# The out-projection as seven products per block pair, with weight sums prepared early in DRAM

## Chip, cores and metric

One core of a Trainium2 chip runs the whole kernel. The metric is the device time of one execution in microseconds (us); less is better. The engines are TensorE (PE, with its weight loads shown apart as PEld), VectorE (DVE), ScalarE (ACT), GpSimd (POOL) and SyncE (SP), from whose queue all DMAs are issued here.

## What is computed

One layer of a hybrid decoder: 2048 tokens of width 1024, an input projection shared by two head groups (8 heads of latent attention, and a gated linear recurrence, HGRN2), gates, one output projection, residual and a final RMSNorm.

```python
h = rms_norm(x, ln_g[l])
proj = h @ w_in[l]
q_lat, kv_lat, k_rope, g_mla, hq, hf, hi, g_hg = jnp.split(proj, split_pts, axis=-1)
y_mla = mla_group(...) * jax.nn.silu(g_mla)        # causal attention, (2048, 512)
y_hg = hgrn2_group(...) * jax.nn.silu(g_hg)        # chunkwise recurrence, (2048, 512)
y = jnp.concatenate([y_mla, y_hg], axis=-1) @ w_out[l]     # (2048, 1024) @ (1024, 1024)
x = x + y
return rms_norm(x, final_norm_g)
```

All is float32. A large matmul is made of three: each operand is split into a high part (a cast to the fp32r type) and a low part (the rest), and high x high, high x low and low x high are accumulated in PSUM (`mm3`, lines 67 to 70).

## The kernel before

Three stages follow one another. **Stage 1** (to about 700 us) projects and runs HGRN2: token chunks of 512, feature groups of 256 columns; each `hg_unit` (line 440) has a first level, five more levels, `inter`, `outputs` and `norm`. A level subtracts on POOL (L447, L468), takes exponentials on ACT (L470, L471), multiplies on DVE (L480, L481) and ends in small matmuls (L486). The latent projections `lat_q` (L249) and `lat_kv` (L314) are merged with the second half of the units: `merge` (L140) spreads the items of its lists evenly over one another, and `merge(U[7:], lat_q(0, hA))` (L658), `merge(U[16:], lat_kv(0, hA))` (L666) and `merge(U[16:], lat_q(1, hB))` (L673) are the places that the change adds to.

**Stage 2** is attention: 8 heads of 8 steps of 256 queries. The loop at L1026 merges, in step n, the scores of step n + 1 (`stage_a`, L859: three matmuls per chunk, row minimum on DVE, exponential on ACT), the transposes and value products of step n (`stage_b`, L905: four transposes into a PSUM bank, cast on ACT L932, subtraction on DVE L933, products L947 and L948), and the preparation of the next head (`prep`, L778, by a plan by hand at L989 to L1002). Each step stores its 64 rows of `y` to DRAM (L962). In the step of number 4 of the last head (`WOUT`, L38) `load_wout` (L974) closes the pool `lat` of the latents and splits `w_out` into the room: 4 loads of 1 MB, per 128 rows a cast on ACT (L984) and a subtraction on POOL or DVE (L985).

**Stage 3** is the out-projection (L1042 to L1079): 16 blocks of 128 tokens. A block loads 512 KB of `y` (L1047), splits it (L1048, L1049), loads `x` (L1051), and for each half of 512 columns runs 8 x 3 matmuls into a PSUM bank; DVE adds the residual (L1062), ACT squares with a sum (L1063), POOL takes the power (L1072), ACT scales one half (L1073), DVE the other (L1074), and SP stores 512 KB (L1079). The last block's second half is cut in two.

The program is written in this order, but a scheduler that goes by the order of writing as priority and by its own time estimates sets the order on each engine, so that work of a later place can stand among the work of an earlier one: out-projection matmuls do so from 1224 us on. PSUM has 8 banks: 3 `mm`, 3 `tp`, 1 `a`, 1 `b`.

Of the kernel before, what the change touches and what calls it, by code (L numbers as in the profile page):

```python
# [57 lines left out]
def hybrid_kernel(ctx: ExitStack, tc: tile.TileContext, x, x_t, positions, ln_g, w_in, q_a_norm_g, w_q_b,  # L58
# [719 lines left out]
    def prep(h):  # L778
# [52 lines left out]
        def query(c):  # L831
# [5 lines left out]
            qf = wk.tile([128, 512], F32, tag="qf", bufs=1, name="qf")  # L837
# [1 line left out]
            qh = wk.tile([128, 512], F32R, tag="qh", bufs=2, name="qh")
            ql = wk.tile([128, 512], F32R, tag="ql", bufs=2, name="ql")  # L840
# [133 lines left out]
    def load_wout():  # L974
        p2r.close()
        wo = p2r.enter_context(tc.tile_pool(name="wo", bufs=1, side="right"))
        for k2 in range(KT // 2):
            wr = wk.tile([128, 2, D], F32, tag="vp", name="vp")
            DMA.dma_start(wr, w_out[k2 * 256:(k2 + 1) * 256, :].rearrange("(k p) n -> p k n", p=128))
            for j in range(2):  # L980
                k = 2 * k2 + j
                a = wo.tile([128, D], F32R, name=f"wo_hi{k}")
                b = wo.tile([128, D], F32R, name=f"wo_lo{k}")
                A.copy(a, wr[:, j])  # L984
                (V if k == 0 else G).tensor_tensor(b, wr[:, j], f32(a), ALU.subtract)  # L985
                w_hi.append(a)
                w_lo.append(b)
# [123 lines left out]
```

## Time and profile before

| | us |
|---|---|
| median of 3 runs (lowest, highest) | 1419.92 (1417.84, 1420.91) |
| the profiled execution, its own time | 1418.87 |
| its span, first to last instruction | 1417.1 |
| PE busy in it | 1387.7 |
| DVE, ACT, POOL busy | 958.6, 881.2, 464.8 |
| mean granted TensorE clock | 0.990 |

The page gives busy time, not useful work: a matmul's listed duration is a latency, and matmuls overlap, so a rate is read from how many start in a stretch, or from the distance of two equal events. What bounds a stretch is read from which engine is full there and which one waits.

### The profile page before, as it was taken

What the parts mean: (1) busy time and instruction counts of PE and PEld (TensorE: products, weight loads), DVE (VectorE), ACT (ScalarE), POOL (GpSimd) and SP (SyncE); (2) the same over time, 40 slices, a digit from 0 to 9 for tenths busy, and PEclk for the clock granted to TensorE, in tenths of its full rate; (3) what the DMA queues carried; (4) which work ended last, traced back from release to release, by engine and by line L of the source; (5) the groups of instructions that cost most, each with busy time, mean ns of one, the idle gap of its engine ahead of it and who ended that gap; (6) DMA issues with size and microseconds to landing.
All of it is one profiled execution on the core that took longest, in us unless ns stands there. A gap on an engine that the chain in (4) does not pass through costs nothing.

```text
span 1417.1 us, 25792 instructions
## 1 busy us (share of the span) xinstructions
PE 1387.7 (98%) x9258; PEld 1263.5 (89%) x9258; DVE 958.6 (68%) x2425; ACT 881.2 (62%) x1796; POOL 464.8 (33%) x635
## 2 busy tenths in 40 slices
PE   8999999999999999999899999999999999999998
PEld 7899879989899988998889898999999998888887
DVE  6547855595845845658388889898889889743333
ACT  6565575456862647355388778778777878732232
POOL 3123613083121622237252425233342525411010
PEclk9999999999999999999989999999999999999999
DMA  7211211215411112111630000100010103244442
GB/s 230 75 48 46 75 53 31 67 42 172 138 46 34 54 52 82 38 42 44 194 73 18 19 22 13 24 13 22 13 26 11 25 22 107 74 144 143 134 148 104
DMA packets 100576, 96.30 MB, mean 68 GB/s; under 512 B 31200, under 2 KB 88800, under 8 KB 100320
## 3 DMA queue, kind: packets, MB, share of 16 engines
q1 hardware_dynamic: 100448, 94.65, 22.7%
q8 instruction: 73, 1.20, 0.4%
q14 instruction: 55, 0.45, 0.1%
HBM read 68.41 MB, written 25.17 MB: 66 GB/s over the span
## 4 chain that ended last, share of the span: by engine, by line
PE 85%; DVE 5%; POOL 3%; ACT 2%; issue 2%; DMA 2%; SPq 0%; POOLq 0%; DVEq 0%; ACTq 0%
PE ps_mm L68 14%; PE ps_mm L69 14%; PE ps_mm L70 14%; PE ps_tp L929 8%; PE ps_a L948 5%; PE ps_a L947 4%; PE ps_mm L881 4%; PE ps_mm L883 4%; PE ps_mm L882 4%; PE ps_b L70 2%; PE ps_b L68 2%; PE ps_b L69 2%; PE ps_a L486 2%; PE ps_b L486 1%; POOL dd L468 1%
## 5 line engine op out<-in xcount | busy, mean ns | idle before, releaser
L68 PE MATMUL ps_mm<-w,hh 128*128 128x256 f32 (+3 forms) x896 | 268.3, 299 | 0.0
L69 PE MATMUL ps_mm<-w,hh 128*128 128x256 f32 (+3 forms) x896 | 263.9, 295 | 0.0
L70 PE MATMUL ps_mm<-w,hl 128*128 128x256 f32 (+3 forms) x896 | 263.0, 294 | 0.0
L933 DVE TENSOR_TENSOR pl<-ps_tp,ph 128x512 fp32r<-128x512 f32 (+1 forms) x288 | 184.6, 655 | 33.3 <-ACT ph L932 32.6
L932 ACT CAST ph<-ps_tp 128x512 fp32r<-128x512 f32 (+1 forms) x288 | 154.4, 565 | 60.2 <-PE ps_tp L929 46.7
L68 PEld LDWEIGHTS ps_mm<-w,hh 128*128 128x128 f32 x896 | 170.1, 190 | 0.7
L69 PEld LDWEIGHTS ps_mm<-w,hh 128*128 128x128 f32 x896 | 169.8, 189 | 0.4
L70 PEld LDWEIGHTS ps_mm<-w,hl 128*128 128x128 f32 x896 | 169.3, 189 | 0.1
L929 PE MATMUL ps_tp<-ident,sn 128*128 128x128 f32 x1088 | 167.9, 274 | 0.8 <-ACT sn L895 0.8
L895 ACT ACTIVATE sn<-sn,mx 128x128 f32<-128x128 f32 (+15 forms) x128 | 154.6, 1208 | 21.2 <-DVE mx L890 20.8
L947 PE MATMUL ps_a<-ph,vp 128*128 128x256 f32 x576 | 155.5, 290 | 0.0
L948 PE MATMUL ps_a<-pl,vp 128*128 128x256 f32 x576 | 147.1, 288 | 0.2 <-DVE pl L933 0.2
L468 POOL TENSOR_TENSOR dd<-G 128x512 f32<-128x512 f32 x80 | 92.8, 1164 | 142.9 <-DVE qd L481 106.9
L929 PEld LDWEIGHTS ps_tp<-ident,sn 128*128 128x128 f32 x1088 | 126.8, 140 | 8.8 <-ACT sn L895 1.3
L881 PE MATMUL ps_mm<-k_hi,qh 128*128 128x512 f32 (+3 forms) x320 | 130.8, 409 | 0.5 <-DVE mx L890 0.2
L886 DVE TENSOR_SCALAR_CACHE_REDUCE sn<-ps_mm,mx 128x512 f32<-128x512 f32 (+3 forms) x192 | 111.5, 581 | 10.9 <-PE ps_mm L883 8.8
L883 PE MATMUL ps_mm<-k_hi,ql 128*128 128x512 f32 (+3 forms) x320 | 116.5, 364 | 1.4 <-DVE ql L842 1.4
L882 PE MATMUL ps_mm<-k_lo,qh 128*128 128x512 f32 (+3 forms) x320 | 116.1, 363 | 0.0
L914 POOL TENSOR_SCALAR gp<-gate,ri 128x64 f32<-128x64 f32 x128 | 56.7, 445 | 180.9 <-DVE ri L897 159.7
L230 DVE SCALAR_TENSOR_TENSOR w<-wr,lng,w 128x256 fp32r<-128x256 f32 (+3 forms) x168 | 89.3, 574 | 39.4 <-ACT w L229 39.4
L948 PEld LDWEIGHTS ps_a<-pl,vp 128*128 128x128 f32 x576 | 109.0, 189 | 6.0 <-DVE pl L933 1.2
L947 PEld LDWEIGHTS ps_a<-ph,vp 128*128 128x128 f32 x576 | 108.9, 189 | 5.8 <-ACT ph L932 0.6
(275 smaller groups left out, 3348.5 us busy)
## 6 DMA issues: line engine op xcount, KB each, us to landing
wr<-in_w_in SPq DMA_DIRECT2D x68, 256.0 KB
yl<-y_d SPq DMA_DIRECT2D x16, 512.0 KB
vp<-in_x SPq DMA_DIRECT2D x16, 512.0 KB
out<-sn SPq DMA_DIRECT2D x15, 512.0 KB
xt<-in_x SPq DMA_DIRECT2D x8, 512.0 KB
xs<-in_x_t SPq DMA_DIRECT2D x8, 512.0 KB
y_d<-yt SPq DMA_DIRECT2D x16, 256.0 KB
gate<-gate_d SPq DMA_DIRECT2D x8, 512.0 KB
```

What stands on the lines that cost most here:

```text
L68: PE.matmul(ps, l_hi, r_hi, start=start, stop=False)
L69: PE.matmul(ps, l_hi, r_lo, start=False, stop=False)
L70: PE.matmul(ps, l_lo, r_hi, start=False, stop=stop)
L881: PE.matmul(p[:, :w], qh[:, qs], kh[:, ks], start=True, stop=False)
L882: PE.matmul(p[:, :w], qh[:, qs], kl[:, ks], start=False, stop=False)
L883: PE.matmul(p[:, :w], ql[:, qs], kh[:, ks], start=False, stop=True)
L895: A.activation(sn[:, :nk], sn[:, :nk], AF.Exp, bias=mx[:, kc:kc + 1], scale=-1.0, accum_out=rs)
L929: PE.transpose(tp[:, o:o + 128], prow[i][:, (kb + u) * 128:(kb + u + 1) * 128], ident)
L932: A.copy(ph[:, :w], tp[:, :w])
L933: V.tensor_tensor(pl[:, :w], tp[:, :w], f32(ph[:, :w]), ALU.subtract)
L947: PE.matmul(dst, vv, ph[:, rng], start=st_, stop=False)
L948: PE.matmul(dst, vv, pl[:, rng], start=False, stop=en)
```

## The change

The 2048 x 1024 by 1024 x 1024 product is taken in pairs of token blocks. For a pair, y is seen as a 2 x 2 matrix of [128 tokens, 512 features] quarters a11, a12 (first block), a21, a22 (second), and w_out as four 512 x 512 quarters b11 to b22. Strassen's scheme in Winograd's form takes seven products in place of eight, with four sums of the left quarters (s1 to s4) and four of the right (t1 to t4).

- `wout_sums` computes and splits the seven right operands in eight pieces in stage 1 (lines 658, 666 and 673 get a third list) and stores them to seven DRAM tensors of 2 MB. It uses the buffers `xs` (3) and `xt` (2) of that stage.
- `load_wout` is gone. From step 3 of the last head on (`WOUT = 3`) the sets are loaded into the room of `lat`: one in each of steps 3, 4 and 6, two in step 5; the last two go, in the last step, into the room of the pool `big`, which now also holds the key, query and value buffers of attention and is closed there.
- Stage 3 has 8 pairs. `pair_operands` loads 1 MB of y and 1 MB of x per pair and makes the seven left operands; `pair_products` runs seven products of 4 x 3 matmuls, accumulating in four PSUM banks (three `mm`, one `tp`) that stay open; two are seeded by an ACT copy from another bank, and one matmul each opens banks b and c once.
- The output is formed in place in the x tile.

```diff
-WOUT = 4
+WOUT = 3
...
+    SETS = ("b11", "t1", "t2", "b21", "t3", "b22", "t4")
+    w_d = {name: dram.tile([128, 2, 4, 512], F32R, name="wd_" + name) for name in SETS}
...
+    def wout_sums(kk, ch):
+        ns = slice(ch * 256, ch * 256 + 256)
+        wr = st.tile([128, 2, 2, 256], F32, tag="xs", bufs=3, name="ws")
+        for g in range(2):
+            r0 = g * 512 + kk * 128
+            DMA.dma_start(wr[:, g], w_out[r0:r0 + 128, :].rearrange("p (c n) -> p c n", c=2)[:, :, ns])
+
+        def split(src, names):
+            hl = st.tile([128, 2, 2, 256], F32R, tag="xs", bufs=3, name="whl")
+            n = len(names)
+            A.copy(hl[:, 0, :n], src)
+            V.tensor_tensor(hl[:, 1, :n], src, f32(hl[:, 0, :n]), ALU.subtract)
+            for i, name in enumerate(names):
+                DMA.dma_start(f32(w_d[name][:, :, kk, ns]), f32(hl[:, :, i]))
+
+        t = st.tile([128, 4, 256], F32, tag="xt", name="xt")
+        G.tensor_tensor(t[:, 0], wr[:, 0, 1], wr[:, 0, 0], ALU.subtract)
+        G.tensor_tensor(t[:, 1], wr[:, 1, 1], t[:, 0], ALU.subtract)
+        G.tensor_tensor(wr[:, 0, 1], wr[:, 1, 1], wr[:, 0, 1], ALU.subtract)
+        G.tensor_tensor(t[:, 2], wr[:, 1, 0], t[:, 1], ALU.subtract)
+        split(wr[:, :, 0], ("b11", "b21"))
+        split(wr[:, :, 1], ("t3", "b22"))
+        split(t[:, 0:2], ("t1", "t2"))
+        split(t[:, 2:3], ("t4",))
+
+    sums = [lambda kk=kk, ch=ch: wout_sums(kk, ch) for kk in range(4) for ch in range(2)]
...
-    merge(U[7:], lat_q(0, hA))
+    merge(U[7:], lat_q(0, hA), sums[0:3])
...
-    merge(U[16:], lat_kv(0, hA))
+    merge(U[16:], lat_kv(0, hA), sums[3:6])
...
-    merge(U[16:], lat_q(1, hB))
+    merge(U[16:], lat_q(1, hB), sums[6:8])
...
+    ORDER = (("a11", "b11", "a"), ("s1", "t1", "e"), ("s2", "t2", "b"), ("a12", "b21", "a"),
+             ("s3", "t3", "b"), ("s4", "b22", "c"), ("a22", "t4", "b"))
+    def wload(pool, name):
+        wset[name] = pool.tile([128, 2, 4, 512], F32R, name=name + "s")
+        DMA.dma_start(f32(wset[name]), f32(w_d[name]))
...
+        def split(name, src):
+            hi, lo = o[name] = operand(name)
+            A.copy(hi, src)
+            V.tensor_tensor(lo, src, f32(hi), ALU.subtract)
...
+        def total(name, x0, x1, op):
+            t = o["f" + name] = fin.tile([128, 4, 128], F32, tag="ss", bufs=3, name="ss")
+            V.tensor_tensor(t, x0, x1, op)
+            split(name, t)
...
-        if n == (HEADS - 1) * STEPS + WOUT:
+        first = n - ((HEADS - 1) * STEPS + WOUT)
+        if first == 0:
             run(side)
-            side = []
-            load_wout()
+            side = [open_wout, early("b11")]
+        elif first > 0 and n < len(seq) - 1:
+            side = side + [early(name) for name in {1: ("t1",), 2: ("t2", "b21"), 3: ("t3",)}[first]]
+        elif n == len(seq) - 1:
+            side = [open_late] + pair_operands(0)[:4] + [late("b22"), late("t4")]
...
+    acc = {"a": mmb(), "e": mmb(), "b": mmb(), "c": tpb()}
+    for key_ in "bc":
+        PE.matmul(acc[key_], wset["b11"][:, 0, 0, 0:128], wset["b11"][:, 0, 0], start=True, stop=True)
...
+        def product(i, ns=slice(0, 512)):
+            a, w, bk = ORDER[i]
+            (ah, al), wt, p = o[a], wset[w], acc[bk][:, ns]
+            for k in range(4):
+                first = i < 2 and k == 0
+                PE.matmul(p, ah[:, k], wt[:, 0, k, ns], start=first, stop=False, skip_group_check=True)
+                PE.matmul(p, ah[:, k], wt[:, 1, k, ns], start=False, stop=False, skip_group_check=True)
+                PE.matmul(p, al[:, k], wt[:, 0, k, ns], start=False, stop=k == 3, skip_group_check=True)
...
+        def after(i):
             if i == 0:
+                A.copy(acc["b"], acc["a"])
+            elif i == 1:
+                add(0, H1, acc["e"])
+                add(1, H1, acc["e"])
+            elif i == 2:
+                A.copy(acc["c"], acc["b"])
+            elif i == 3:
+                add(0, H0, acc["a"])
+                done(0, H0, True)
+            elif i == 4:
+                add(1, H1, acc["b"])
+                done(1, H1, True)
+            elif i == 5:
+                add(0, H1, acc["c"])
+                done(0, H1, False)
+                finish(0, H0, H1)
+            elif not last:
+                add(1, H0, acc["b"])
+                done(1, H0, False)
+                finish(1, H1, H0)
```

Here `add` is the DVE addition of a bank to the x tile, `done` the square with its sum and, for one half, the multiplication by the final gain, `finish` power, scaling and store.

## Rows read from the trace of the kernel before

**Rows 1.** The page, part 1: busy time, share, instructions.
```profile
PE 1387.7 (98%) x9258; PEld 1263.5 (89%) x9258; DVE 958.6 (68%) x2425; ACT 881.2 (62%) x1796; POOL 464.8 (33%) x635
```
**Rows 2.** The page, part 4: the last chain's shares by engine.
```profile
PE 85%; DVE 5%; POOL 3%; ACT 2%; issue 2%; DMA 2%; SPq 0%; POOLq 0%; DVEq 0%; ACTq 0%
```
**Rows 3.** Out-projection: busy time by stretch (columns above it); SP's store issues.
```profile
core 0: us, PE busy (x) PEld busy (x) DVE busy (x) ACT busy (x) POOL busy (x), PEclk, DMA share, GB/s
1300.00:1350.00 50.00, 50.00 (x222) 41.38 (x222) 18.08 (x27) 14.72 (x28) 5.22 (x9) 1.00 0.44 142
...
1305.05 0.34 SPq L1079 DMA_DIRECT2D out<-sn  x1
...
1315.93 0.34 SPq L1079 DMA_DIRECT2D out<-sn  x1
```
**Rows 4.** Busy time by stretch, HGRN2 beside latent projections; columns as in rows 3.
```profile
140.00:160.00 20.00, 18.22 (x138) 17.84 (x137) 19.20 (x40) 12.64 (x38) 16.24 (x20) 0.91 0.08 27
160.00:180.00 20.00, 20.00 (x137) 16.93 (x136) 11.09 (x28) 9.71 (x25) 7.96 (x13) 1.00 0.36 106
...
300.00:320.00 20.00, 17.39 (x140) 15.73 (x138) 18.41 (x36) 10.17 (x31) 16.63 (x23) 1.00 0.14 48
...
475.00:495.00 20.00, 18.67 (x153) 18.16 (x153) 17.62 (x42) 10.98 (x33) 16.42 (x19) 1.00 0.12 41
```
**Rows 5.** One of three matmul lines, both banks: ns min/median/max, first and last start.
```profile
L68 PE MATMUL ps_mm<-wo_hi,yh x176: 278/389/481, 1224.1 to 1407.5; 128*128 128x512 f32 x168, 128*128 128x256 f32 x8
...
L68 PE MATMUL ps_b<-wo_hi,yh x88: 283/389/397, 1249.1 to 1410.4; 128*128 128x512 f32 x80, 128*128 128x256 f32 x8
```
**Rows 6.** Groups by line over the span: busy us, mean ns, idle before.
```profile
L814 POOL TENSOR_TENSOR vp<-vs,vp 128x256 fp32r<-128x256 f32 x24 | 17.4, 737 | 21.8 <-ACT vp L813 21.8
...
L841 ACT CAST qh<-qf 128x512 fp32r<-128x512 f32 x32 | 19.9, 622 | 0.7 <-DVE qf L838 0.6
...
L1062 DVE TENSOR_TENSOR vp<-ps_mm,vp 128x512 f32<-128x512 f32 (+1 forms) x22 | 14.9, 676 | 25.1 <-PE ps_mm L70 23.8 <-DMA vp<-in_x 1.2
...
L1074 DVE SCALAR_TENSOR_TENSOR sn<-vp,rxp,ks 128x512 f32<-128x512 f32 x16 | 12.0, 751 | 10.8 <-POOL rxp L1072 10.8
L1067 DVE TENSOR_TENSOR vp<-vp,ks 128x512 f32<-128x512 f32 x16 | 11.1, 692 | 15.4 <-ACT sn L1063 15.4
```
**Rows 7.** One tile's instructions, w_out's halves: ns min/median/max, first and last start.
```profile
L984 ACT CAST wo_hi<-vp x8: 1044/1051/1057, 1185.4 to 1220.2; 128x1024 fp32r<-128x1024 f32 x8
L985 POOL TENSOR_TENSOR wo_lo<-vp,wo_hi x7: 2393/2405/2474, 1187.5 to 1222.7; 128x1024 fp32r<-128x1024 f32 x7
L985 DVE TENSOR_TENSOR wo_lo<-vp,wo_hi x1: 1225/1225/1225, 1186.5 to 1186.5; 128x1024 fp32r<-128x1024 f32 x1
```
**Rows 8.** Busy time by stretch, attention; last, of instructions on tile yh alone (no POOL).
```profile
1100.00:1150.00 50.00, 50.00 (x344) 45.87 (x343) 42.90 (x140) 41.83 (x91) 22.84 (x32) 1.00 0.12 30
...
1187.00:1197.00 10.00, 9.13 (x52) 6.78 (x50) 9.85 (x29) 9.63 (x18) 7.53 (x7) 1.00 0.63 192
...
1224.00:1262.00 38.00, 38.00 (x221) 33.12 (x219) 17.77 (x35) 16.62 (x35) 5.96 (x9) 1.00 0.24 76
...
1224.00:1262.00 38.00, 24.65 (x76) 13.75 (x77) 1.23 (x1) 1.69 (x2) 1.00 0.24 76
```
**Rows 9.** POOL's and DVE's timelines, 144 to 149 us; one line's ns min/median/max.
```profile
144.15 3.66 POOL L468 TENSOR_TENSOR dd<-G 128x512 f32<-128x512 f32 x3
...
144.16 0.41 DVE L481 TENSOR_TENSOR qd<-rq,dd 128x256 f32<-128x256 f32 x1
...
146.79 1.30 DVE L481 TENSOR_TENSOR qd<-rq,dd 128x256 f32<-128x256 f32 x1
...
L481 DVE TENSOR_TENSOR qd<-rq,dd x80: 407/417/1311, 81.5 to 651.9; 128x256 f32<-128x256 f32 x80
```
**Rows 10.** Busy time by stretch while w_out is loaded; columns as in rows 3.
```profile
1178.00:1181.00 3.00, 3.00 (x21) 2.67 (x20) 2.34 (x11) 2.85 (x8) 2.05 (x5) 1.00 0.92 289
```
**Rows 11.** Timeline at the end: the last matmul and the last store's issue.
```profile
1410.63 0.28 PE L70 MATMUL ps_b<-wo_hi,yl 128*128 128x256 f32 x1
...
1413.95 0.38 SPq L1076 DMA_DIRECT2D out<-sn  x1
```

More of the change, by code (lines that the diff above doesn't have):

```diff
@@ L767, in hybrid_kernel @@
     wk = p2.enter_context(tc.tile_pool(name="wk", bufs=2, side="left"))
-    big = p2.enter_context(tc.tile_pool(name="big", bufs=1, side="left"))
     wk2 = p2.enter_context(tc.tile_pool(name="wk2", bufs=2, side="left"))
+    fin = p2.enter_context(tc.tile_pool(name="fin", bufs=1, side="left"))
+    p2k = ExitStack()
+    big = p2k.enter_context(tc.tile_pool(name="big", bufs=1, side="left"))
     k_hi1 = big.tile([128, S], F32R, name="k_hi1")
@@ L836, in query @@
                 mm3(p, wqh[:, k], wql[:, k], q_hi[:, k, sl], q_lo[:, k, sl], k == 0, k == 1)
[L837 removed]
+            qf = big.tile([128, 512], F32, tag="qf", bufs=1, name="qf")
             V.tensor_tensor(qf, p, csT[:, sl], ALU.mult)
[L839 to L840 removed]
+            qh = big.tile([128, 512], F32R, tag="qh", bufs=2, name="qh")
+            ql = big.tile([128, 512], F32R, tag="ql", bufs=2, name="ql")
             A.copy(qh, qf)
@@ L972, in hybrid_kernel @@
     w_hi, w_lo = [], []
-    def load_wout():
-        p2r.close()
[L976 to L987, printed above, removed]
+    ORDER = (("a11", "b11", "a"), ("s1", "t1", "e"), ("s2", "t2", "b"), ("a12", "b21", "a"),
+             ("s3", "t3", "b"), ("s4", "b22", "c"), ("a22", "t4", "b"))
@@ new lines, in hybrid_kernel, with open_wout @@
+    wset = {}
+    ys = [{} for _ in range(NBLK // 2)]
+    o_pools = {}
+    def wload(pool, name):
+        wset[name] = pool.tile([128, 2, 4, 512], F32R, name=name + "s")
+        DMA.dma_start(f32(wset[name]), f32(w_d[name]))
+    def open_wout():
+        p2r.close()
+        o_pools["wo"] = p2r.enter_context(tc.tile_pool(name="wo", bufs=1, side="right"))
+        o_pools["fng"] = fng = fin.tile([128, D], F32, name="fng")
+        DMA.dma_start(fng, bass.AP(tensor=final_norm_g.tensor, offset=final_norm_g.offset, ap=[[0, 128], [1, D]]))
@@ new lines, in early, with open_late, late, operand @@
+    def early(name):
+        return lambda: wload(o_pools["wo"], name)
+    def open_late():
+        p2k.close()
+        o_pools["ln"] = ln.enter_context(tc.tile_pool(name="ln", bufs=1, side="right", reuse_waits="tile"))
+    def late(name):
+        return lambda: wload(o_pools["ln"], name)
+    ln = ExitStack()
+    def operand(name):
+        if name in ("a11", "s1", "s2", "a12"):
+            t = o_pools["ln"].tile([128, 2, 4, 128], F32R, tag=name, name=name)
+            return t[:, 0], t[:, 1]
+        if name in ("s3", "s4"):
+            t = wk2.tile([128, 2, 4, 128], F32R, tag="gate", name="gate")
+            return t[:, 0], t[:, 1]
+        return (wk2.tile([128, 4, 128], F32R, tag="ph", bufs=3, name="ph"),
+                wk2.tile([128, 4, 128], F32R, tag="pl", bufs=3, name="pl"))
@@ L1081, in hybrid_kernel @@
+    run(pair_operands(0)[4:])
+    for b in range(NBLK // 2):
+        merge(pair_products(b), pair_operands(b + 1) if b + 1 < NBLK // 2 else [])
+    ln.close()
+    p2.close()
     p2r.close()
-    p2.close()
 def kernel(x, positions, ln_g, w_in, q_a_norm_g, w_q_b, kv_a_norm_g, w_kv_b, hg_lower_bounds, hg_norm_g,
```

104 lines of the change are left out of this document (63 added, 41 removed).

## Prediction

> **What bounds the kernel now.** I read the busy table of the whole span first, then the shares of the chain that ended last, then busy time by stretch, and last the single rows that price an edit. TensorE is busy 98% of the span and carries 85% of the chain, DVE and POOL 8% together [rows 1, 2]. So the time is TensorE's work plus the few places where it is kept waiting, and an edit is worth what it takes from TensorE's queue or adds to those places. The out-projection is the purest case: in a 50 us stretch TensorE never stops at full clock, while DVE is busy 18 us, ACT 15 us, and DMA a share of 0.44 [rows 3]. There two stores of finished blocks are issued 10.88 us apart [rows 3], and a block is 2 halves x 8 tiles x 3 matmuls = 48 of 512 columns: 0.2267 us each. (The listed 389 ns is a pipelined latency, not a price.)
>
> The places where TensorE is kept waiting matter for what the change adds. In the HGRN2 stage there are stretches, about 140 to 160, 300 to 320 and 475 to 495 us, where it is busy only 17.4 to 18.7 of 20 us while DVE is busy 17.6 to 19.2 and POOL 16.2 to 16.6; 20 us later it is full again and DVE has fallen to 11 [rows 4].
>
> **The change, part by part.**
>
> *Out-projection.* Before, 248 matmuls of 512 columns and 16 of 256 start from each of three lines [rows 5]: 744 and 48, worth 768 of the long ones (16 blocks x 48). After, 8 block pairs x 7 products x 4 tiles x 3 = 672, plus 2 that only open two banks. That takes 94 away: 94 x 0.2267 = **-21.3 us**, all on the path, since nothing else bounds this stage. What must still fit in a pair's 84 x 0.2267 = 19.0 us: DVE does 7 subtractions and 4 operand sums of two SBUF tiles (11 x 0.69), 6 additions out of PSUM (6 x 0.68), 2 multiplications (2 x 0.69), 2 final scalings (2 x 0.75) and two tiny steps: 14.9 us. ACT does 7 casts, 2 bank copies, 4 squares and 2 scalings, 15 x 0.62 = 9.3 us [rows 6]. DMA moves 3 MB per pair as before. DVE goes from 37% to 78%, and TensorE stays the bound.
>
> *Bank copies.* Two copies PSUM to PSUM per pair are new (a to b after product 1, b to c after product 3), and TensorE waits for each. No row shows such a copy; the nearest is a cast at 0.62 us [rows 6]. One whole product, 12 x 0.2267 = 2.7 us, lies between each copy's source and its reader, so I cost them at nothing; uncovered they cost 8 x 2 x 0.62 = 9.9 us. The two additions that must empty bank b (after products 5 and 7) have the same 2.7 us of cover.
>
> *w_out preparation in attention.* Gone from head 7's steps: 8 casts of 1.05 us on ACT, 7 subtractions of 2.41 us on POOL, 1 of 1.2 us on DVE, 4 loads [rows 7]. In 1187 to 1197, where these and the first two blocks' operands ran, TensorE was busy 9.13 of 10 us, where a plain attention stretch gives 50 of 50 [rows 8]. The seven 2 MB loads that replace it go straight to their place and need no engine. I take **-1.5 us** (0, if another wait takes the place, to -2.5 us with the sparser queue of that stretch).
>
> *Weight sums.* Eight pieces: 3 beside the first lat_q, 3 beside the first lat_kv, 2 beside the second lat_q. Each is 4 POOL operations of 128x256, 3 casts of 128x512 and one of half that on ACT, the same number of subtractions on DVE, 2 loads of 256 KB and 7 x 2 stores of 128 KB on SP. POOL: 4 x 0.737 = 2.95 us. ACT: 3.5 x 0.62 = 2.2 us. DVE: 3.5 x 0.69 = 2.4 us [rows 6]. In all 23.6, 17 and 19 us. The HGRN2 units they sit beside need DVE and POOL in turn, in exactly the stretches of rows 4. From the merge positions (1/6, 3/6, 5/6 of a list; 1/4, 3/4 for the pair) about 4 of 8 pieces fall into such a stretch, the others where DVE has 8 us of 20 free. Queued behind each piece's ops are the next unit's decay products, and behind those TensorE's small level matmuls. Four pieces x 2.4 us of DVE are 9.8 us; TensorE still has projection matmuls to run meanwhile, so I take **+6 us**, between 0 (all beside other work) and 23.6 (POOL's whole time comes through). The three-buffer ring (one load, four split tiles per piece) makes each piece wait for the stores of the one before; those 16 SP issues stand ahead of the next weight loads, which are prefetched, and I put nothing on it beyond this range.
>
> DVE and POOL do not overlap freely here: a DVE product of 128x256 with both inputs in SBUF takes 0.41 us at 144.2, and 1.30 us at 146.8 while POOL runs three operations until 147.8; over 80 such products the minimum is 407 ns, the median 417, the maximum 1311 [rows 9]. The Trainium skill (SBUF — State Buffer, "Who interferes with whom") states this as an exclusive lock: a VectorE instruction with two SBUF inputs and a GpSimd instruction that reads SBUF fully block each other. The row agrees; by that rule POOL's and DVE's time of a piece add up, which speaks against this change and is the first rival below.
>
> *Handover from attention.* Before, out-projection matmuls filled attention's last 38 us: 76 of two of the three lines, so 114, or 25.8 us, in 1224 to 1262, TensorE never idle [rows 8]; attention's own rest was 12 us. After, the operand pool opens only when the last scores have let the key and query buffers go, which is the same moment, 1224. Product 1 needs just one split (a cast and a subtraction, 1.3 us), and 4 products (11 us) can run before bank c, one of the three transpose banks, is needed. From 1224 on DMA owes the first pair 1 MB of y and 1 MB of x and the last two sets of 2 MB. At 289 GB/s, the rate while w_out was loaded [rows 10], 6.3 MB take 22 us: all there at 1248, and set 6 is due at 1224 + 12 + 5 x 2.7 = 1249.5. That is close. I take **+1 us** (0 to +6).
>
> *End.* From the last matmul at 1410.6 to the span's end at 1417.1 the steps stay the same (addition, square, power, scaling, two half stores) [rows 11]: 0.
>
> **Sum.** -21.3 - 1.5 + 6 + 1 = -15.8. From the profiled execution's 1418.87 us (span 1417.1 and 1.8 around it) that is 1403.1; the median of the runs shown lies 1.05 above that execution, so **1404 us**.
>
> **Rivals.**
>
> 1. *The weight sums block both engines (ends slower).* Place: the three stretches of rows 4. If TensorE waits out POOL's and DVE's time of every piece one after the other, the price is 8 x (2.95 + 2.4) = 43 us: -21.3 - 1.5 + 1 + 43 = +21, **1441 us**. From 2.7 us of lost TensorE time per piece on, the change loses. For it: DVE at 19.2 of 20 and the 1.30 us row. Against it: only half of the pieces lie there, and before the change TensorE lost no more than 1.3 to 2.6 us of 20 in these stretches with all their collisions. Chance 0.05. With POOL's time alone, 23.6, it comes to +1.8, **1422 us**, no change that can be told: 0.06.
>
> 2. *The handover starves.* If the last two sets come at 190 GB/s instead of 289 (6.3 MB in 33 us, set 7 at 1259 where it is due at 1252), and the second pair's y load, which needs the value buffer that the last attention product frees, is not there when the first pair ends, the handover costs +10 in place of +1: -6.8, that is **1413 us**. For it: seven sets are 10 MB more than w_out's 4. Against it: DMA runs at a share of 0.24 there [rows 8]. Chance 0.12.
>
> 3. *The sums cost nothing and attention gains its full 2.5 us*: -23.8, **1396 us**. For it: TensorE's explicit waits in those stretches are short. Chance 0.12.
>
> 4. *The products do not flow*: the bank copies queue behind DVE's 78% and ACT, and the seven-product stage doesn't do what it says; 9.9 us come back, **1414 us**. Against it: 2.7 us of cover each. Chance 0.04.
>
> **Chances.** Forecast 0.61, its own range 1398 to 1410; rivals 0.05 and 0.06, 0.12, 0.12, 0.04. Faster by over 0.2%: 0.61 + 0.12 + 0.12 + 0.04 = 0.89; within 0.2% (some 2.8 us, about what a measurement of this kernel can tell from no change): 0.06; slower 0.05. The range 1396 to 1414 leaves out rival 1 in both its sizes and the outer edges of rivals 2 to 4: at most 0.2.
>
> **What would show it.** Right: three groups of out-projection matmuls of 224 or so each (two of them less records lost), stores 19.0 us apart per pair with TensorE full in between; TensorE busy about as before in 140 to 180, 285 to 330 and 470 to 515, each stretch of the stage ending 1 to 3 us later; 1187 to 1224 without waits; no wait on sets b22 and t4. Wrong: TensorE waiting on DVE or ACT in each pair (rival 4), DVE rows of 1.2 us and more lined up under POOL's new operations with the next projection starting over 3 us late per piece (rival 1), or a gap on a DMA behind the last score (rival 2).

## The result, and the profile after

| | before | after |
|---|---|---|
| median of 4 runs each, us | 1420.41 | 1444.37 (1439.6 to 1447.08) |
| the profiled execution, its span | 1418.87, 1417.1 | 1444.27, 1441.9 |
| mean granted TensorE clock | 0.990 | 0.984 |

The change makes the kernel slower: the ratio is 1.016, 95% interval 1.0139 to 1.018. The forecast was 1404 us with a range to 1414.

Part 1 (busy time) and part 4 (the last chain's shares) of the changed kernel's page:

```profile
PE 1386.1 (96%) x9152; PEld 1253.5 (87%) x9152; DVE 1028.5 (71%) x2544; ACT 913.0 (63%) x1876; POOL 481.7 (33%) x660
...
PE 58%; DMA 4%; DVE 3%; ACT 2%; POOL 1%; issue 1%; SPq 0%; POOLq 0%; ACTq 0%; DVEq 0%
```

These shares can't be set beside those of [rows 2] as they stand. They add up to 69% of the span, those of before to 99%, because this chain is followed back only to 416 us; its first piece (start, us, what):

```profile
416.10 0.48 ACT rq L382
```

TensorE's 58% is thus 84% of what is covered, against 86% before. What can be told is that DMA has 4% of the span though the first 416 us are missing, and had 2% before: waits for transfers have come into the path. To find where, I take four TensorE instructions that both kernels have: the first key product (end of stage 1), the 70th of 320 score products (attention in its steady part; it starts at 820.3 us before and at 847.4 after), the last score product, and the last matmul. The other three stand in these views of a tile or a line (changed kernel; duration ns min/median/max, first and last start):

```profile
L68 PE MATMUL ps_b<-c_hi,wk_hi x16: 390/393/793, 718.3 to 1154.6; 128*128 128x512 f32 x16
...
L914 PE MATMUL ps_mm<-k_hi,qh x320: 222/399/522, 738.0 to 1261.2; 128*128 128x512 f32 x112, 128*128 128x384 f32 x32, 128*128 128x128 f32 x8, 128*128 128x256 f32 x8
...
L1152 PE MATMUL ps_mm<-t4s,ph x36: 279/394/399, 1289.2 to 1434.9; 128*128 128x512 f32 x28, 128*128 128x256 f32 x8
L1152 PE MATMUL ps_mm<-t1s,s x32: 389/393/475, 1264.4 to 1399.5; 128*128 128x512 f32 x32
L1152 PE MATMUL ps_mm<-t2s,s x32: 389/389/632, 1271.1 to 1422.0; 128*128 128x512 f32 x32
```

The last matmul starts at 1435.1 (1410.6 before, [rows 11]). Stretch by stretch:

| stretch | before, us | after, us | difference | forecast |
|---|---|---|---|---|
| start to first key product | 698.7 | 718.3 | +19.6 | +6 (sums) |
| to the 70th score product | 121.6 | 129.1 | +7.5 | 0 |
| to the last score product | 402.7 | 413.8 | +11.1 | -1.5 |
| to the last matmul | 187.6 | 173.9 | -13.7 | -20.3 |
| all four | 1410.6 | 1435.1 | +24.5 | -15.8 |

**Stage 1.** The eight pieces of the weight sums do not run at their places in the lists. Six start at 22 to 108 us and two at 388 to 408: they wait for nothing but a buffer, and the scheduler takes what can go. Busy time by stretch (columns as in rows 3), the early part and then the three stretches that answer to rows 4, each later by 15 or 20 us:

```profile
70.00:80.00 10.00, 8.34 (x30) 6.74 (x31) 7.98 (x16) 8.40 (x16) 2.06 (x2) 0.83 0.89 269
...
90.00:100.00 10.00, 6.84 (x36) 5.71 (x35) 4.83 (x10) 5.47 (x11) 5.40 (x6) 0.94 0.51 162
100.00:110.00 10.00, 8.26 (x55) 7.95 (x55) 7.04 (x13) 8.50 (x16) 3.27 (x3) 0.72 0.82 216
...
155.00:175.00 20.00, 18.03 (x136) 17.41 (x135) 19.73 (x41) 12.46 (x38) 16.24 (x20) 0.91 0.08 27
...
315.00:335.00 20.00, 18.71 (x139) 17.26 (x137) 18.41 (x36) 10.16 (x30) 16.54 (x23) 0.91 0.13 46
495.00:515.00 20.00, 18.63 (x153) 18.15 (x153) 17.61 (x43) 10.98 (x32) 16.10 (x18) 1.00 0.12 41
```

The stretches of rows 4 lose no more than before. The early ones lose 1.7 to 3.2 us of 10 and were full before, as two of them show in the kernel before:

```profile
70.00:80.00 10.00, 10.00 (x45) 8.11 (x44) 1.97 (x4) 8.81 (x11) 0.00 (x0) 1.00 0.26 71
90.00:100.00 10.00, 10.00 (x87) 10.00 (x86) 3.98 (x8) 7.47 (x14) 3.35 (x3) 1.00 0.30 75
```

The granted clock of the changed kernel reads 0.83, 0.94 and 0.72 of full there: part of the time TensorE has the lower of its two levels (1.2 in place of 2.4 GHz), so a gap costs more than itself. In 70 to 80 us 30 matmuls start where 45 did, a third fewer, though TensorE is busy only a sixth less. Waits in 55 to 125 us (us in total, times, longest):

```profile
DVE whl L628 <- ACT whl L627: 15.1, 11, 3.7
ACT whl L627 <- DMA ws<-in_w_out: 8.2, 3, 4.1
...
PE ps_mm L68 <- ACT w L231: 4.2, 2, 3.0
...
PE ps_mm L70 <- DVE w L232: 2.2, 1, 2.2
...
ACT w L231 <- DMA wr<-in_w_in: 0.6, 1, 0.6
```

and SP's own in 20 to 125 us:

```profile
SPq L630 <- DVE whl L628: 41.1, 13, 10.8
```

TensorE waits for weights (`w`). ACT and DVE, which split them, stand waiting inside the pieces (`whl`), and SP, which loads them, stands before the pieces' stores (L630). The weights' own loads are hardly late (0.6 us), so DMA traffic is not what keeps them from TensorE. I call loss how much later the same matmul starts than in the kernel before: it is 14.4 us at 107 us, stays near that until the last two pieces at 388 to 408, and is 19.6 from 420 us on. Of the 14.4, some 8 are TensorE's explicit waits (the two above and 1.7 us in L69) and some 5 the lower clock (an estimate: 10 us times the 0.17, 0.06 and 0.28 that the clock lacks in the three stretches).

**Into attention.** One wait of TensorE is 11.1 us and ends at 736 (waits in 715 to 765); in the kernel before it was 2.1 us (the last line, waits in 680 to 735 there):

```profile
PE ps_b L68 <- ACT ks L859: 11.1, 1, 11.1
...
ACT ks L859 <- DMA gate_d<-gt: 3.5, 1, 3.5
```

```profile
PE ps_b L68 <- ACT ks L826: 2.1, 1, 2.1
```

SP's timeline there:

```profile
722.63 7.74 SPq L822 DMA_DIRECT2D gate<-gate_d  x2
730.46 2.11 SPq L368 DMA_DIRECT2D gate_d<-gt  x1
```

The last gate store of stage 1 (L368) is queued behind two issues of a load for attention, which keep SP for 7.7 us, and ACT may not write `ks` before that store is through.

**End of attention.** All five early sets are issued within 3 us from 1212.6 on. The next 64 KB store of attention's output comes behind them, in the chain (start, us, what):

```profile
1217.66 25.61 DMA y_d<-oa
```

Busy time by stretch there:

```profile
1230.00:1240.00 10.00, 9.47 (x47) 6.92 (x47) 8.62 (x32) 6.28 (x9) 1.34 (x3) 1.00 1.01 428
1240.00:1250.00 10.00, 6.27 (x33) 5.84 (x33) 2.54 (x6) 4.61 (x10) 1.17 (x2) 0.66 0.18 66
```

The store lands after 25.61 us; `oa` has two buffers, so the next output can't leave PSUM, and TensorE drops to 6.27 of 10 at a granted clock of 0.66 (its longest wait there, 3.7 us, is for DVE's sum into `oa`).

**Out-projection.** In its middle it does what was forecast. A stretch of it:

```profile
1310.00:1360.00 50.00, 50.00 (x218) 40.62 (x217) 37.28 (x63) 23.64 (x49) 6.83 (x10) 1.00 0.46 166
```

SP's timeline, in which the stores of a pair run together (the last row spans two pairs):

```profile
1337.81 5.25 SPq L1187 DMA_DIRECT2D out<-sn  x2
...
1357.18 5.26 SPq L1187 DMA_DIRECT2D out<-sn  x2
1376.55 24.34 SPq L1187 DMA_DIRECT2D out<-sn  x4
```

The two bank copies by line (busy us, mean ns):

```profile
L1191 ACT COPY ps_mm<-ps_mm 128x512 f32<-128x512 f32 x8 | 4.6, 575 | 0.5 <-PE ps_mm L1154 0.5
L1196 ACT COPY ps_tp<-ps_mm 128x512 f32<-128x512 f32 x8 | 4.6, 572 | 15.5 <-PE ps_mm L1154 15.4
```

A pair takes 19.4 us with TensorE full, where two blocks took 21.8 [rows 3]. In two of the eight pairs TensorE waits for the first copy: in the second (its timeline, with the wait in brackets) and in the last (waits in 1410 to 1436):

```profile
1298.17 0.50 PE L1152 MATMUL ps_mm<-t2s,s 128*128 128x512 f32 x1 [1.44 <-ACT ps_mm L1191]
...
PE ps_mm L1152 <- ACT ps_mm L1191: 1.8, 1, 1.8
```

### The profile page after: what moved, and what is told of

It is laid out like the page before. It is cut to its first block, busy times and chain, and to the rows that moved or that the text cites. A ratio compares the mean times of both kernels' runs of the same rounds, so it can differ in the third digit from the quotient of the medians.

```text
span 1441.9 us, 25928 instructions
## 1 busy us (share of the span) xinstructions
PE 1386.1 (96%) x9152; PEld 1253.5 (87%) x9152; DVE 1028.5 (71%) x2544; ACT 913.0 (63%) x1876; POOL 481.7 (33%) x660
## 4 chain that ended last, share of the span: by engine, by line
PE 58%; DMA 4%; DVE 3%; ACT 2%; POOL 1%; issue 1%; SPq 0%; POOLq 0%; ACTq 0%; DVEq 0%
PE ps_tp L962 8%; PE ps_mm L68 5%; PE ps_mm L69 5%; PE ps_mm L70 5%; PE ps_a L981 5%; PE ps_a L980 4%; PE ps_mm L914 4%; PE ps_mm L915 4%; PE ps_mm L916 4%; PE ps_mm L1152 3%; PE ps_mm L1153 3%; PE ps_mm L1154 3%; DMA y_d<-oa 2%; DMA vp<-y_d 1%; DMA q_lo<-latq_d 1%
## 5 line engine op out<-in xcount | busy, mean ns | idle before, releaser
L68 PE MATMUL ps_mm<-w,hh 128*128 128x256 f32 (+3 forms) x896 | 270.9, 302 | 3.5 <-ACT w L231 3.3
L69 PE MATMUL ps_mm<-w,hh 128*128 128x256 f32 (+3 forms) x896 | 267.2, 298 | 3.3 <-DVE w L232 3.1
L68 PEld LDWEIGHTS ps_mm<-w,hh 128*128 128x128 f32 x896 | 172.4, 192 | 4.8 <-ACT w L231 3.7
L69 PEld LDWEIGHTS ps_mm<-w,hh 128*128 128x128 f32 x896 | 172.1, 192 | 4.9 <-DVE w L232 4.4
L928 ACT ACTIVATE sn<-sn,mx 128x128 f32<-128x128 f32 (+15 forms) x128 | 154.6, 1208 | 28.3 <-DVE mx L923 27.9
L470 POOL TENSOR_TENSOR dd<-G 128x512 f32<-128x512 f32 x80 | 93.9, 1180 | 108.8 <-DVE qd L483 78.5
```

The costliest lines, as they stand in the source:

```text
L68: PE.matmul(ps, l_hi, r_hi, start=start, stop=False)
L69: PE.matmul(ps, l_hi, r_lo, start=False, stop=False)
L928: A.activation(sn[:, :nk], sn[:, :nk], AF.Exp, bias=mx[:, kc:kc + 1], scale=-1.0, accum_out=rs)
```

## Experiments

All start from the changed kernel. Medians are of one chip's runs, and before ran beside each (1419.4 to 1420.9). The four columns on the right are the stretches of the table above, as differences to before in the profiled execution. A first version of e12_nosums, e1_no_sums, gave no time.

| run | median us | ratio to before, 95% | stage 1 | into att. | att. | out-proj. |
|---|---|---|---|---|---|---|
| changed kernel | 1444.4 | 1.014 to 1.018 | +19.6 | +7.5 | +11.1 | -13.7 |
| e12_nosums | 1422.3 | 1.001 to 1.003 | -1.4 | +7.0 | +10.6 | -15.4 |
| e2_pinned | 1453.7 | 1.021 to 1.025 | +27.9 | +10.5 | +11.6 | -13.4 |
| e6_poolq | 1443.9 | 1.014 to 1.020 | +19.0 | +8.2 | +11.3 | -13.2 |
| e8_slack | 1453.4 | 1.022 to 1.025 | +28.9 | +8.1 | +11.1 | -13.6 |
| e11_gpin | 1441.4 | 1.013 to 1.017 | +19.4 | +6.4 | +10.9 | -13.6 |
| e16_poolall | 1442.7 | 1.014 to 1.017 | +19.2 | +9.4 | +11.5 | -13.5 |
| e3_ks_first | 1444.2 | 1.014 to 1.019 | +20.3 | +7.2 | +11.3 | -13.6 |
| e7_tilewaits | 1439.1 | 1.012 to 1.015 | +19.4 | +3.2 | +10.7 | -13.6 |
| e9_oa6 | 1434.0 | 1.009 to 1.012 | +18.7 | +5.5 | +0.3 | -10.2 |
| e10_paced | 1440.7 | 1.013 to 1.016 | +19.9 | +5.2 | +0.1 | -5.5 |
| e21_yqueue | 1444.8 | 1.016 to 1.021 | +18.6 | +5.6 | +11.4 | -11.5 |
| e13_combo | 1436.2 | 1.010 to 1.014 | +19.2 | +3.8 | +0.2 | -7.8 |
| e15_bound | 1412.7 | 0.994 to 0.997 | -0.3 | +4.6 | +0.3 | -10.4 |
| e14_best | 1424.2 | 1.001 to 1.003 | +16.0 | +3.5 | +0.1 | -12.8 |
| e20_best5 | 1426.0 | 1.002 to 1.004 | +13.8 | +3.3 | +0.2 | -10.5 |
| e19_best4 | 1429.2 | 1.004 to 1.007 | +14.5 | +7.3 | +0.1 | -11.8 |
| e17_best2 | 1431.6 | 1.006 to 1.009 | +15.5 | +9.8 | +0.3 | -12.5 |
| e18_best3 | 1448.2 | 1.017 to 1.022 | +30.7 | +8.3 | +0.2 | -12.2 |

### What the sums cost

e12_nosums leaves the sums out and fills the sets from one small tile, so that it does not compute the layer:

```diff
-    sums = [lambda kk=kk, ch=ch: wout_sums(kk, ch) for kk in range(4) for ch in range(2)]
+    sums = [lambda name=name: fill(name) for name in SETS]
```

> The weight sums' loads, sums and splits are left out (the sets hold a constant pattern): their seven stores of 2 MB to DRAM, from one small tile, and everything after them stay. Theory (the sums' engine work and their place cost the 19.6 us by 718 us): 1425 us (1422 to 1428), TensorE full in 60-120. Rival (part of it is the stores' 15 MB or the new layout): over 1431.

1422.3, and stage 1 is back (-1.4). The sums with their loads, splits and waits cost 22 us. The run still stores the seven sets, but at 124 to 152 us, so by itself it does not clear the early transfers; the 0.6 us above does. e6_poolq takes the stores off SP's queue:

```diff
-                DMA.dma_start(f32(w_d[name][:, :, kk, ns]), f32(hl[:, :, i]))
+                G.dma_start(f32(w_d[name][:, :, kk, ns]), f32(hl[:, :, i]))
```

> The 56 stores of the sums are issued on GpSimd's queue in place of SP's; nothing else is changed. Theory (SP's queue: stores that wait for DVE's subtractions, 41 us of waits in 20-125 us, stand ahead of the next weight loads): most of the early 14.9 us goes, the later 4.7 stays: about 1432 us (1429 to 1436). Rival (the engines: DVE's and ACT's shares of the sums stand ahead of the operand splits that TensorE waits for): no change, 1442 to 1447.

No change: at 107 us the loss is 7.5 in place of 14.4, but at 127 it is 14.2. To free SP's queue is not enough. The run does not tell what part that queue has, because it also gives GpSimd the 56 issues, at 0.8 to 1.0 us each (0.6 on SP).

e2_pinned and e8_slack tie each piece's load to a later tile (`pin`, the last decay product or projection; the line shown is e2's):

```diff
         wr = st.tile([128, 2, 2, 256], F32, tag="xs", bufs=3, name="ws")
+        V.tensor_copy(wr[:, :, 0, 0:1], pin[-1][:, 0:2].unsqueeze(2))
```

> All sums stay, but each piece's w_out load now waits for the last decay product written before its place in the HGRN2 stage (a 2-element VectorE copy into its buffer), so no piece can start before that stretch. Theory (the cost is that of the early stretch, where weights are still being loaded and TensorE has no slack): the early 14.9 us go, and the pieces cost at their place what I first put on them, 0 to 23.6 with +6: about 1431 us (1425 to 1437). Rival (a piece costs TensorE about 2.4 us wherever it runs, by DVE's and POOL's time): 1444. Second rival (in the HGRN2 stage, where DVE is full, they cost more, up to 43): 1455 to 1468.

> All sums stay; each piece's w_out load waits (a 2-element ScalarE copy) for a feature-major projection, so the pieces run 2, 3 and 3 beside the projections at about 240-280, 420-460 and 580-620 us, where before DVE was busy 5.5 to 8 of 20 us and POOL 0 to 1, in place of 22-119 us (changed kernel) or beside the decay products (e2_pinned, 27.9 us lost by 700 us). Theory (TensorE loses by the sums only where DVE and POOL have no slack): nearly all of the 19.6 us goes, 1444.4 - 19.6 = 1425 us (1423 to 1430). Rival (a piece costs 2.4 us or more wherever it is): 1444 or over.

Both missed their forecasts (1431 and 1425) and are worse than the early place: 27.9 and 28.9 us by the end of stage 1, some 3.5 a piece. e8 did not test what it was meant to: the projections it waits for are fillers among the HGRN2 units, and the pieces ran at 187 to 231, 397 to 435 and 535 to 589 us. e11_gpin ties them to the last projection group of each set (`pin` is the copy of a gate projection):

```diff
-    merge(U[:16], vv + gg)
+    merge(U[:16], beside(vv + gg, sums[0:3]))
```

> All sums stay; each piece now waits for one of the gate projections' copies (hg_proj's last group), so 3, 3 and 2 pieces run at about 255-277, 441-465 and 595-615 us, where before DVE is busy 5.5 to 6.6 of 20 us and POOL 0 to 1. In e8_slack they had not run there: the projections they waited for are fillers, and the pieces ran at 187-234, 400-420 and 505-573, beside the decay products. Theory (a piece costs TensorE time only where DVE, ACT and POOL have none to spare): 1444.4 - 19.6 + 0 to 5 = 1425 to 1430 us. Rival (a piece costs 2.4 to 3.5 us wherever it runs): 1444 to 1453.

The sum is as bad (+19.4), but the pieces are not alike. Stretches of e11:

```profile
255.00:285.00 30.00, 29.57 (x253) 28.54 (x253) 16.71 (x34) 12.63 (x26) 7.07 (x9) 1.00 0.59 185
285.00:300.00 15.00, 10.20 (x65) 9.94 (x64) 9.45 (x15) 10.33 (x22) 10.47 (x13) 0.83 0.58 206
```

POOL's first operation of the three pieces:

```profile
261.32 0.74 POOL L635 TENSOR_TENSOR xt<-ws 128x256 f32<-128x256 f32 x1 [5.94 <-DMA ws<-in_w_out]
...
272.74 0.74 POOL L635 TENSOR_TENSOR xt<-ws 128x256 f32<-128x256 f32 x1 [7.80 <-DMA ws<-in_w_out]
...
287.42 0.73 POOL L635 TENSOR_TENSOR xt<-ws 128x256 f32<-128x256 f32 x1 [11.15 <-DMA ws<-in_w_out]
```

The second of these stretches in the kernel before:

```profile
285.00:300.00 15.00, 15.00 (x119) 15.00 (x118) 13.57 (x26) 8.55 (x23) 13.89 (x16) 1.00 0.05 16
```

Two pieces in 257 to 284 cost TensorE 0.4 us of busy time in 30 (the loss grows by 1.1). The third, among the decay products, costs 4.8 of 15, while DVE and POOL are busy less than before (9.45 for 13.57, 10.47 for 13.89). The waits in 284 to 300 show why:

```profile
PE ps_tp L534 <- DVE qt L509: 4.8, 1, 4.8
...
DVE whl L630 <- ACT whl L629: 4.3, 1, 4.3
```

TensorE's whole 4.8 us are one wait, for a DVE product of the HGRN2 units (`qt`). Ahead of that product DVE stands 4.3 us in a step of the piece, waiting for ACT's cast, which in turn needs the piece's load, and runs two of the piece's subtractions. Pieces start 11 to 15 us apart though each needs only 7.6 of engine time, because its steps pass between SP, POOL, ACT and DVE; whatever is queued behind a waiting step waits too.

e16_poolall puts casts, subtractions and stores of a piece on GpSimd, so that ACT and DVE have no step in it:

```diff
-            A.copy(hl[:, 0, :n], src)
-            V.tensor_tensor(hl[:, 1, :n], src, f32(hl[:, 0, :n]), ALU.subtract)
+            G.tensor_copy(hl[:, 0, :n], src)
+            G.tensor_tensor(hl[:, 1, :n], src, f32(hl[:, 0, :n]), ALU.subtract)
```

> The sums' casts and subtractions move from ScalarE and VectorE to GpSimd, which also issues their stores; nothing else is changed, so the pieces still start in 22-120 us. Theory (in-order queues: ACT and DVE wait inside a piece for its load, for GpSimd and for each other, with the next weights' splits behind them): with no instruction of a piece left on ACT, DVE or SP but its loads, 10 to 18 of the 22 us go: 1427 to 1435 us. Rival (the engines' time and DVE's sharing with GpSimd, whose part of a piece grows from 3 to some 12 us): 1444 or more.

In total the rival's time, in the early part the theory's. Stretches of e16:

```profile
70.00:80.00 10.00, 10.00 (x44) 7.97 (x43) 6.64 (x9) 9.91 (x15) 5.88 (x9) 1.00 0.78 242
...
90.00:100.00 10.00, 8.38 (x51) 7.57 (x51) 8.71 (x11) 6.84 (x12) 7.88 (x9) 0.83 0.60 169
```

DVE's and POOL's timelines at 101 us:

```profile
101.53 1.64 DVE L482 TENSOR_TENSOR kd<-k,dd 128x256 f32<-128x256 f32 x1
...
101.56 1.31 POOL L470 TENSOR_TENSOR dd<-G 128x512 f32<-128x512 f32 x1
```

By 80 us 1.0 is lost (6.5 in the changed kernel), by 107 us 5.2 (14.4), though with four pieces begun by then in place of six. Later the decay differences (L470) share POOL with the pieces, and the loss goes on to 19.2. The stores weigh there too: their issue, cheap on SP, takes POOL 0.8 us each (ns min/median/max, first and last start):

```profile
L630 POOL DMA_DIRECT2D wd_t<-whl x32: 667/799/1366, 43.5 to 444.8; - x32
```

So a piece takes some 17 us of POOL (an estimate: 11.8 us of operations and 7 x 0.8), not the 12 that the expectation names. A DVE product of 0.41 us takes 1.64 beside POOL's operation, as in rows 9. The Trainium skill (SBUF — State Buffer, "Who interferes with whom") has such a pair block each other in full; the trace agrees. How much of the later loss is that, how much the issues and how much POOL's order was not separated.

### The way into attention

e3_ks_first gives `ks` an address off the gate buffers:

```diff
+    ks0 = big.tile([64, S], F32, tag="ks", bufs=1, name="ks")
     k_hi1 = big.tile([128, S], F32R, name="k_hi1")
```

> In the attention pool the buffer ks is placed first and k_hi1, k_lo1 after it, so ks no longer lies on the gate buffers of stage 1. Theory (TensorE's 11 us wait at 736 us is for ACT's first write to ks, which waits for the last gate store, itself queued behind a gate load on SP): 1444.4 - 7.5 = 1437 us (1435 to 1439). Rival (another buffer or that gate load itself is as late, the wait only changes its name): 1443 to 1446.

No change: ACT's first write to `ks` waits for the same store. e7_tilewaits keeps that and adds waits by buffer in place of the closed pool's whole region, for `wk2`, `fin` and `big`:

```diff
-    big = p2k.enter_context(tc.tile_pool(name="big", bufs=1, side="left"))
+    big = p2k.enter_context(tc.tile_pool(name="big", bufs=1, side="left", reuse_waits="tile"))
```

> e3_ks_first and, for the three attention pools that now lie on stage 1's st and w buffers (wk2, fin, big), waits buffer by buffer in place of the whole region of the closed pool. e3_ks_first showed that moving ks off the gate buffers changes nothing: ACT's first write to ks still waited for the last gate store. Theory (the wait belongs to the pool's whole region, which now holds the gate buffers where before it lay on buffers that were free earlier): without it the wait at 736 us goes, 1444.4 - 7.5 = 1437 us (1434 to 1440). Rival (TensorE then waits for the next thing there, ACT's key copies or the last gate projections): 1442 to 1446.

The stretch costs 3.2 in place of 7.5 and the kernel 1439.1: the wait was the region's, not the buffer's. What is left (waits in 700 to 750):

```profile
PE ps_b L68 <- ACT ks L860: 7.6, 1, 7.6
...
ACT q_hi L760 <- DMA q_lo<-latq_d: 7.2, 3, 2.8
```

ACT's write no longer waits itself; it stands behind ACT's casts of loads that are late. This stretch scatters between runs: 5.2 to 10.5 with the old waits, 3.2 to 4.6 in five of the eight runs with the new ones, but 7.3 to 9.8 in e17 to e19, which stays unexplained. So the gain of 4 holds for e7 beside the changed kernel and is not safe for each neighbour.

### The set loads and the small store

e9_oa6 gives `oa` 6 buffers; e10_paced lets each early set's load wait for the attention output of the step before; e21_yqueue issues the last head's output stores from GpSimd.

```diff
-            tmp = wk.tile([64, 256], F32, tag="oa", name="oa")
+            tmp = wk.tile([64, 256], F32, tag="oa", bufs=6, name="oa")                # e9
+            G.tensor_copy(wset[name][0:64, 0, 0, 0:1], last_y[-1][:, 0:1])            # e10, in wload
+            (G if h == HEADS - 1 else DMA).dma_start(y_d[j // 2][...], tmp)           # e21
```

> The attention output buffer oa gets 6 buffers in place of 2; nothing else is changed. Theory (11 us are lost at 1215-1250 because ACT's next write to oa waits for a 64 KB store that stands behind 10 MB of set loads and lands 25.6 us late): 1444.4 - 11 = 1433 us (1431 to 1437). Rival (another wait on the same transfers, such as the first pair's y load, takes its place): 1441 to 1446.

> Each of the five early set loads waits for a 1-element GpSimd copy of the last attention output written before its step, so that one or two sets are issued per attention step, as the list is written, in place of all five within 3 us. Theory (the y store stands behind too many loads at once): a store then stands behind at most two sets, some 10 us, and ACT's wait goes: 1444.4 - 11 = 1433 us (1431 to 1438). Rival (the late sets move the wait to product 2 to 5 of the first pair): 1440 to 1448.

> In the changed kernel the last head's eight stores of attention output are issued by GpSimd, which also computes their data, in place of SP; oa keeps its two buffers. Theory (the store waits its turn behind the sets on SP's queue): from another queue it lands within some 5 us, ACT's wait goes and with it the 11 us at 1215-1250: 1444.4 - 11 = 1433 us (1431 to 1438). Rival (all queues share the 16 DMA engines, which are full, so it is as late): 1442 to 1447.

e9: the 11 us are gone (stretches):

```profile
1230.00:1240.00 10.00, 10.00 (x75) 9.35 (x74) 8.95 (x30) 7.41 (x14) 1.62 (x3) 1.00 0.90 370
1240.00:1250.00 10.00, 10.00 (x69) 9.06 (x68) 9.66 (x28) 8.15 (x15) 1.63 (x3) 1.00 0.14 30
```

though 3.4 come back in the out-projection. e10 takes the same 11 away, but gives 8 back: `PE ps_mm L1155 <- ACT a L1067` waits 4.0 us for the next pair's y, with DMA still at a share of 0.87 in 1270 to 1290. e21 settles what held the store, in the summary of the tile `oa`, 1200 to 1262:

```profile
DMA to landing us min/median/max: 2.0/2.1/6.5
```

and its waits in 1200 to 1260 show what was next:

```profile
PE ps_a L980 <- DVE oa L992: 7.0, 1, 7.0
DVE ss L1072 <- DMA vp<-y_d: 4.8, 1, 4.8
```

From another queue the slowest of these stores lands after 6.5 us, though two of them are issued while DMA moves 388 to 425 GB/s (1210 to 1230): the 25.6 us were the place behind the sets. The Trainium skill (DMA: Bandwidth & Descriptors, "Queues, rings and completion order") says that a DMA engine takes turns between queues packet by packet; the trace agrees. The time did not change, because now the first pair's y load comes behind the sets on SP's queue (28.85 us in the chain), and DVE, whose first operand sum waits for it, holds `oa` as the store did. The expected 1433 was wrong for that reason.

### Together

e13_combo is e7 and e9, with the second pair's y in a buffer of the scores that is free earlier. e15_bound is e12, e7 and e9 (so without the sums); e14_best is e7 and e9 with two early pieces and two in each of e11's windows; e20_best5 the same with the two early pieces on GpSimd; e19_best4 that again with the windows' pieces started sooner; e17_best2 and e18_best3 are e16 with e7 and e9, the second with e14's windows.

> e7_tilewaits and e9_oa6 together, and the second pair's y goes to a buffer of the scores (free some 40 us earlier than the value buffer it had). Theory (three separate losses: 4.3 to 7.5 at the transition, 10.5 at the set loads, 4 to 7 at the second pair): 1444.4 - 5 - 10.5 - 5 = 1424 us (1419 to 1428). Rival (the second pair then waits for the next thing, set t4 or its operands): 1428 to 1431.

> e12_nosums (the sums' loads, sums and splits left out, the sets hold a constant pattern), e7_tilewaits and e9_oa6 together: what the out-projection by seven products is worth without its three side costs. Theory (the three are separate): 1422.3 - 4.5 - 10 = 1408 us (1404 to 1411), near the 1404 first forecast. Rival (with one gone another takes its place): 1413 to 1420.

> e7_tilewaits and e9_oa6 together; of the eight sums the first two stay where the changed kernel ran them (22-60 us), and two each wait for a gate projection's copy at about 255-280, 452-475 and 605-630 us. In e11_gpin the first two of each window (11 us a piece) cost TensorE 0 to 1.5 us, and the third, which ran on into the decay products, 6.3 us. Theory (a piece costs nothing while projections fill TensorE and nothing that TensorE needs stands behind it in DVE's, ACT's and POOL's order): sums -22 + 7, transition -4.5, set loads -10: 1444.4 - 29.5 = 1415 us (1411 to 1418), faster than before. Rival (a piece costs 2.4 us in any place and the losses move on): 1425 to 1430.

> e14_best with only the first two pieces moved wholly to GpSimd; the windows stay. Theory: e14's 1424.2 less the 2 us that the first two pieces cost less there: 1422 us (1421 to 1424). Rival (GpSimd's longer part of them costs DVE as much): 1424 to 1426.

> e14_best, with the first two pieces wholly on GpSimd (as in e16_poolall, 1 us for both) and the two pieces of each window pinned some 7 to 11 us earlier, behind the last value projection and the first gate projection, so that the second piece ends at about 272, 465 and 617 in place of 285, 475 and 630. Theory (a piece is free where nothing that TensorE needs soon stands behind it on any of its engines): e15_bound's 1412.7 + 1 + 3 x (1 to 2) = 1417 to 1420 us. Rival (the earlier start meets the decay products at 241-256, and a piece costs 2 to 3 us there as everywhere): 1423 to 1428.

> e16_poolall, e7_tilewaits and e9_oa6 together. Theory: e15_bound's 1412.7 plus what e16's pieces still cost, 4 to 12: 1417 to 1425 us. Rival (as in e16): 1428 to 1436.

> e14_best with the sums wholly on GpSimd as in e16_poolall: two pieces early, two each behind a gate projection's copy at about 257, 452 and 605 us, where GpSimd has 0 to 1 of 20 us to do. Theory (nothing of a piece stands in ACT's or DVE's order): 1412.7 + 2 to 5 = 1415 to 1418 us, below the kernel before. Rival (the piece's 12 us of GpSimd stand ahead of the decay differences that follow): 1422 to 1430.

None of the seven came out in the range of its forecast. e13 is no faster than e9 (1.010 to 1.014 against 1.009 to 1.012). The y wait is gone, but waits for the first bank copy take its place (waits in 1225 to 1432):

```profile
PE ps_mm L1154 <- ACT ps_mm L1193: 7.0, 3, 3.2
```

e15, without the sums, is 7.3 us faster than before: that is what seven products are worth here with the sums and the loss at the set loads gone, and 4.6 us still lost on the way into attention. With the sums nothing came below the kernel before; e14 is nearest at 1.0023. In e14 the two early pieces cost 3.1 us and the windows 4.6, 5.5 and 2.8 (the second piece runs on into the decay products), against e15's -0.3 for all of stage 1. An earlier start (e19; 7 to 11 us were meant, measured against the matmuls beside them the loads come 5 to 6 us sooner) made the second and third windows nearly free (1.0 and 1.7) and the first dearer (8.8), so some 5 us of shift decide. e17 and e18 have all of a piece on GpSimd, some 17 us of that engine's time; that this meets the decay differences, as in e16, is argued and not shown.

## Why the prediction was wrong

**Out-projection, right, with its handover too small.** 94 matmuls fewer and 19.4 us a pair (19.0 forecast). The stage gained 13.7 where -21.3 + 1 was due. Of the missing 6.6, some 2.6 lie in the pairs themselves: 19.37 us each in place of 84 x 0.2267 = 19.04, eight times, with TensorE full; why a matmul costs 0.2306 us there was not asked. The rest lies at two places, at 1290 to 1300 and at 1418.8, and at both TensorE waits mainly for a bank copy, which I cost at nothing. A copy takes 0.575 us (0.62 forecast), but the step that failed is that a whole product lies between its source and its reader: that holds in six of eight pairs. In the second pair only two matmuls of product 2 had run in between, and the copy stood on ACT behind a cast that waited for a y load (11.96 us from issue to landing in the chain; the late y of rival 2). In the last, product 2 had already run a pair earlier (last `t1s` at 1399.5, last `t2s` at 1422.0), so nothing was left between, and the copy stood behind a square of ACT that waited for DVE. This is rival 4's mechanism, in two pairs. The explicit waits there are 1.4 and 1.8 us; the lower clock after each gap makes up part of the rest. (In the handover's sum 1224 + 22 is 1246, not 1248; no set was waited for.)

**w_out preparation.** "The seven 2 MB loads that replace it go straight to their place and need no engine" was a step that failed. I priced what the loads need and not what is queued behind them on SP: -1.5 became +11, which e9 takes away and e21 puts down to the place in the queue.

**Weight sums, the largest miss.** 22 us by e12 against +6; the bound of 23.6 covered it by luck, with an argument that does not hold. I put the pieces at their merge positions, though they depend on nothing and the order on each engine comes from a scheduler; six of the eight ran at 22 to 119 us. The second false step was to price a piece by engine time (2.4 to 3 us on its slowest engine) against spare time. e11 shows two pieces nearly free with idle engines and no decay work behind them, and 5 us lost to one wait behind a step of the third, where DVE and POOL were less busy than before: the price is the wait that its chain puts ahead of others in four queues. Rival 1 had the sign right and the place wrong: the stretches of rows 4 lose no more than before. That its 1441 us lies near the measured time is luck, since it has nothing for the other two losses; how much the two engines block each other where the pieces ran was not separated. In rows 9 I passed over that POOL is at work from 144.15 on, so the product at 144.16 took its 0.41 us beside it. The sums' stores are 7 of 256 KB a piece, not 14 of 128 KB, so the bytes are right and the issues too many; and rival 3 leaves out its own +1 (-22.8, 1397 us).

**Into attention.** There was no term. The diff moves `ks` to a pool that takes stage 1's gate buffers, and I read it as a change of place only: +7.5, of which e7 gives back 4, within the scatter of this stretch.

**End.** 6.8 us from the last matmul to the span's end, 6.5 before: right.

The three side costs (the sums' chains, the pool's region, the store behind the sets) add to 38 us against the out-projection's 14. From the forecast's -15.8 to +24.5 the sums make up 13.6 us, the way into attention 7.5, the set loads 12.6 and the out-projection 6.6. Of the queues that the change moves work past I looked at SP's for the sums' stores alone.

## What to carry to other kernels

Before pricing moved work, ask what holds it at its place: work without a dependency runs as early as its buffers allow, and a chain that hops over four engines is priced by its length and by what stands behind each hop, not by its busy time. A large prefetch has to be checked against the small transfers that follow on its queue and the number of their buffers. When a pool moves in SBUF, look up whose region it now takes, since the first write to it may wait for all of that.

## What the hardware showed unexpectedly

Behind 10 MB on the same queue a 64 KB store took 25.6 us, from another queue at most 6.5 beside the same loads. A copy from PSUM bank to PSUM bank by ACT takes 0.575 us for 128x512, a cast from SBUF 0.62. TensorE's clock read 0.66 to 0.83 of full in stretches of 10 to 15 us whose longest single wait was 3.0 to 4.8 us. Issuing a 256 KB store took 0.6 us on SP and 0.8 to 1.0 us on GpSimd.
